# Second token group loads stored low parts of weights, and attention operands take a way through DRAM, in a hybrid decoder layer on one core

## The chip, the cores and the metric

The kernel runs on one core of one Trainium2 chip. The metric is the time of one execution in microseconds (us) on the device.

## What is computed

One decoder layer over 1024 tokens of width 1024 in float32. The part around the change is the mixer: an RMS norm, one projection by `w_in`, four heads of retention and four heads of differential attention, and an output projection. After it comes an expert layer that chooses 16 of 16384 experts for each token and each of eight heads.

```python
h = rmsnorm(x, norm_mix_g); proj = h @ w_in
rq, rk, rv, rg, dq, dk, dv = split(proj)            # dq, dk: 4 heads x 2 maps x 64 columns
q, k as (T, head, map m, 64);  q *= 64 ** -0.5
p_m = softmax(q_m @ k_m.T + alibi, causal);  dy = (p_0 - lam * p_1) @ dv
x = x + concat(silu(rg) * rmsnorm(retention), rmsnorm(dy) * g) @ w_out
x = rmsnorm(x + peer(rmsnorm(x), wq, subkeys, u, v))
```

## The kernel before

The 1024 tokens are eight tiles of 128. `front` runs the mixer and the routing for two groups of tiles after each other: the first group has three tiles (the sparse group: its experts are gathered row by row), the second has five (the dense group: all experts are multiplied). Both groups need the same 52 weight chunks of 128x1024 float32 (512 KB each): 16 for the projections to q and k of the heads (`wt`), 12 to values and gates (`wn`), 8 of `w_out` (`wo`), 16 of the query weights of the routing (`wq`).

Products keep nearly full float32 precision by splitting both factors into a rounded high part and the remainder, the low part, and adding three products. `chunk` (L149) makes the parts of a weight chunk: SyncE (SP) loads `wraw` into one of four buffers (L152), ScalarE (ACT) copies it to the high part `whi` (L154), VectorE (DVE) subtracts to the low part `wlo` (L156). High and low parts have two buffers each (tags `uh` and `ul`). `proj_t` (L168) multiplies a chunk into one PSUM bank (tag `T`, one buffer): 24 matmuls of 384 columns for the first group; for the second 24 matmuls of 320 columns for each of two halves of the tokens, so that the second half waits until the first is read out of the bank. `proj_n` (L178) does the projections whose output has the tokens on the partitions.

For each attention head h, `att_proj` (L295) takes two chunks. A projected half goes to `pt` (one buffer; L300, L316). For q, ACT makes two high parts and their copies in the other 64 partitions (L303, L304) and DVE four low parts (L305, L306): `qa0`, `qa1`, `qb0`, `qb1`. For k, ACT makes the high part (L319) and DVE puts the low part into the other 64 partitions (L320): `kk`. The first group stores its keys to `kd_d` (L323), and the second loads them from GpSimd's (POOL's) queue (L312). `attention` (L327) then handles one tile t after the other: score matmuls `psS` (L343 to L348) into two banks, maxima on DVE (L351, L353), exponentials on ACT (L357), the difference of the two maps on DVE (`e`, L362), transposes `psA` (L369), copies `aT` (L370) and the product with the values `pov` (L373).

L379 to L384 weave the heads: while the tiles of head h run, the four chunks of head h+1 (two of `ret_proj`, L255, whose `qT` is kept in one of two `ga` buffers until the retention of that head is done, and two of `att_proj`) are written in between. While the second group runs, POOL gathers expert rows for the first group (L862), each followed by a multiply on DVE (L864); the place of these on DVE is held back by the list `gates`.

The order of the instructions on each engine is set when the program is built, by a scheduler that weighs program order, free buffers and its own model of durations. At run time every engine, and SP with its transfers, goes through its list strictly in that order, and waits at an instruction whose inputs or buffers aren't ready. A transfer that reads DRAM waits on SP until the store of those bytes has landed.

Of the kernel before, what the change touches and what calls it, by code (L numbers as in the profile page):

```python
# [13 lines left out]
F32 = mybir.dt.float32  # L14
F32R = mybir.dt.float32r
# [4 lines left out]
AF = mybir.ActivationFunctionType  # L20
ALU = mybir.AluOpType
AX = mybir.AxisListType

P = 128
T = 1024
# [3 lines left out]
H = 4  # L29
# [69 lines left out]
def layer_kernel(ctx, tc, x, wt, wn, wo, wq, sk, ut, u, v, gmix, gffn, gfin, gsub, dlam, consts, alb, out):  # L99
# [6 lines left out]
    kd_d = tc.dram_tile([H, 2, P, T], F32, name="kd_d")  # L106
# [27 lines left out]
    def front(m, pp, cst, g0, nt, dense, late):  # L134
# [14 lines left out]
        def chunk(src, shape):  # L149

            raw = wp.tile(shape, F32, tag="raw", bufs=RAW, name="wraw")
            SY.dma_start(raw, src)  # L152
            hi = wp.tile(shape, F32R, tag="uh", bufs=2, name="whi")
            A.activation(hi, raw, AF.Copy)  # L154
            lo = wp.tile(shape, F32R, tag="ul", bufs=2, name="wlo")
            V.tensor_sub(lo, raw, hi.bitcast(F32))  # L156
            return hi, lo
# [83 lines left out]
        yield from proj_n([wn[c] for c in range(4)], hx, lambda t, ps: A.activation(rv[:, t], ps, AF.Copy))  # L241
        yield from proj_n([wn[8 + c] for c in range(4)], hx, put_dv)
# [12 lines left out]
        def ret_proj(h):  # L255
            qT = wp.tile([P, n], F32, tag="ga", bufs=2, name="qT")
            for a, b, ps in proj_t(wt[2 * h], hx):
# [3 lines left out]
            for a, b, ps in proj_t(wt[2 * h + 1], hx):  # L261
                A.activation(kT[:, a:b], ps, AF.Copy, scale=P ** -0.5)
            ops[h] = [qT, kT]
            yield
# [30 lines left out]
        def att_proj(h):  # L295
            qa = [ap.tile([P, n], F32R, tag=f"q2{m}", bufs=2, name=f"qa{m}") for m in range(2)]
            qb = [ap.tile([P, n], F32R, tag=f"qb{m}", bufs=1, name=f"qb{m}") for m in range(2)]
            for a, b, ps in proj_t(wt[8 + 2 * h], hx):
                pt = ap.tile([P, b - a], F32, tag="pt", name="pt")
                A.activation(pt, ps, AF.Copy, scale=0.125)  # L300
                for m in range(2):
                    own, oth = slice(64 * m, 64 * m + 64), slice(64 - 64 * m, 128 - 64 * m)
                    A.activation(qa[m][own, a:b], pt[own], AF.Copy)  # L303
                    A.activation(qa[m][oth, a:b], pt[own], AF.Copy)  # L304
                    V.tensor_sub(qb[m][own, a:b], pt[own], qa[m][own, a:b].bitcast(F32))  # L305
                    V.tensor_sub(qb[m][oth, a:b], pt[own], qa[m][own, a:b].bitcast(F32))  # L306
            yield
            kk2 = ap.tile([P, 2, L], F32R, tag="kd", name="kk") if h % 2 else fp.tile([P, 2, L], F32R, tag="R", name="kk")
            kk = [kk2[:, m] for m in range(2)]
            if not first:  # L310
                for m, tl in enumerate(kk):
                    G.dma_start(tl[:, :lo0], kd_d[h, m][:, :lo0])  # L312
            for a, b, ps in proj_t(wt[8 + 2 * h + 1], hx):
                sl = slice(lo0 + a, lo0 + b)
                pt = ap.tile([P, b - a], F32, tag="pt", name="pt")
                A.activation(pt, ps, AF.Copy)  # L316
                for m in range(2):
                    own, oth = slice(64 * m, 64 * m + 64), slice(64 - 64 * m, 128 - 64 * m)
                    A.activation(kk[m][own, sl], pt[own], AF.Copy)  # L319
                    V.tensor_sub(kk[m][oth, sl], pt[own], kk[m][own, sl].bitcast(F32))  # L320
            if not last:
                for m, tl in enumerate(kk):
                    SY.dma_start(kd_d[h, m][:, lo0:L], tl[:, lo0:].bitcast(F32))  # L323
            ops[h] += [qa, qb, kk]
            yield

        def attention(h):  # L327
# [3 lines left out]
            for t in range(nt):  # L331
# [4 lines left out]
                for m in range(2):  # L336
                    ps = bankA("psS") if both is None else both[:, m:m + 1]
                    ql = slice(t * P, (t + 1) * P)
                    for b in range((Lq + 511) // 512):
                        c0, c1 = b * 512, min(Lq, b * 512 + 512)  # L340
                        o = ps[:, b, :c1 - c0]
                        rl = c0 + T - Lq
                        PE.matmul(o, cst["albl"][:, h], cst["albr"][:, rl:rl + c1 - c0], start=True, stop=False)  # L343
                        diag = c1 == Lq
                        PE.matmul(o, qa[m][:, ql], kk[m][:, c0:c1], start=False, stop=False)
                        PE.matmul(o, qb[m][:, ql], kk[m][:, c0:c1], start=False, stop=not diag)
                        if diag:
                            PE.matmul(o[:, c1 - c0 - P:], identb, cst["mask"], start=False, stop=True)  # L348
# [39 lines left out]
        yield from proj_n([wn[4 + c] for c in range(4)], hx,  # L388
# [14 lines left out]
        for hf in range(2):  # L403
            SY.dma_start(x2[hf], x[g0:g0 + nt, :, 512 * hf:512 * (hf + 1)].rearrange("t p d -> p t d"))
            yield from proj_n([wo[4 * hf + c] for c in range(4)], mx,
# [29 lines left out]
        for hp in range(2 * PH):  # L435
            h = hp // 2
            qT = wp.tile([P, n], F32, tag="ga", bufs=2, name="pqT")
            for a, b, ps in proj_t(wq[hp], nx, "TR"):
                A.activation(qT[:, a:b], ps, AF.Copy)
# [471 lines left out]
```

## Time and profile before

| | |
|---|---|
| time, median of 3 runs | 2898.01 us (2894.97 to 2901.68) |
| time of the profiled execution | 2897.35 us |
| its span | 2895.6 us |
| busy: TensorE (PE), DVE, ACT, POOL | 93%, 82%, 37%, 37% of the span |

The span runs from the first instruction to the last; 1.75 us lie around it. A busy PE is not a PE at its peak: the ends of matmuls are modelled, and overlap. By lines, the execution falls into stages: first group's mixer 0 to 183 us, its routing woven with the second group's first projections to 407 us, the second group's retention and attention to some 690 us, its gate and output projections to 820 us, its routing to 1000 us, one-hot gate tables to 1307 us, and from there the expert loop to the end.

### The profile page before, as it was taken

Reading aid. Unit: us, or ns where it says so; the run is one execution under the profiler, and the core shown is the slowest. Engines: PE = TensorE matmul, PEld = TensorE weight load, DVE = VectorE, ACT = ScalarE, POOL = GpSimd, SP = SyncE. Lnnn points to the kernel's source line nnn. Section 1 sums busy time; section 2 is a strip of 40 time slices with the busy share of each in tenths; the row PEclk is TensorE's granted clock in tenths of the full one; section 3 lists DMA queues with packets and bytes.
Section 4 is the critical chain, followed back from the end, with each engine's and each line's share of the span. In section 5 each row is a group of like instructions: output and inputs, shape, how many; then the busy total and the mean of one; then the engine's idle time right before and its main releaser. Section 6 shows DMA issues by size and latency. Waiting matters only on the chain.

```text
span 2895.6 us, 43107 instructions
## 1 busy us (share of the span) xinstructions
PE 2705.9 (93%) x16043; PEld 2437.2 (84%) x16043; DVE 2362.2 (82%) x4547; ACT 1063.1 (37%) x1881; POOL 1067.1 (37%) x782
## 2 busy tenths in 40 slices
PE   7979987888889999998999999999999999999998
PEld 6868876776789999997887787999999999999987
DVE  3555899878689988985888787888889888988988
ACT  4653334544232369992222222222222222222222
POOL 0000004434310000002555554565565566665664
PEclk9989999999989999999999999999999999999999
DMA  5334236757742246668998898989999999999997
GB/s 170 103 131 141 95 114 230 245 191 241 250 147 82 87 153 238 242 258 298 317 324 301 301 340 307 344 314 353 328 330 348 325 344 339 346 329 332 343 325 259
DMA packets 293238, 742.92 MB, mean 257 GB/s; under 512 B 23450, under 2 KB 117658, under 8 KB 293027
## 3 DMA queue, kind: packets, MB, share of 16 engines
q0 software_dynamic: 111744, 404.28, 39.1%
q1 hardware_dynamic: 181282, 335.88, 33.5%
q8 instruction: 126, 2.06, 0.3%
q14 instruction: 86, 0.70, 0.1%
HBM read 671.71 MB, written 68.35 MB: 256 GB/s over the span
## 4 chain that ended last, share of the span: by engine, by line
PE 34%; DVE 15%; DMA 15%; issue 12%; POOL 7%; ACT 3%; SPq 0%; POOLq 0%; DVEq 0%; ACTq 0%
DMA gl<-hs_d 6%; POOL vg L869 5%; DMA vg<-in_v,idx 4%; DMA ug<-in_u,idx 3%; PE psH L717 3%; PE psH L719 3%; PE psH L718 3%; PE psV L795 3%; PE psV L796 3%; PE psV L797 2%; DVE ug L864 2%; PE psHs L717 2%; PE psHs L719 2%; PE psHs L718 2%; POOL ug L862 2%
## 5 line engine op out<-in xcount | busy, mean ns | idle before, releaser
L869 POOL DMA_INDIRECT vg<-in_v,idx x384 | 548.9, 1429 | 895.3 <-DVE ug L864 521.0
L862 POOL DMA_INDIRECT ug<-in_u,idx x384 | 512.8, 1335 | 499.4 <-DVE ug L864 323.5
L871 DVE SCALAR_TENSOR_TENSOR sa<-vg,shs,sa 128x1024 f32<-128x1024 f32 x384 | 491.7, 1280 | 44.0 <-DMA vg<-in_v,idx 39.2
L864 DVE SCALAR_TENSOR_TENSOR ug<-ug,sx 128x1024 f32<-128x1024 f32 x384 | 460.4, 1219 | 71.0 <-DMA ug<-in_u,idx 70.1
L717 PE MATMUL psH<-nh,uh 128*128 128x320 f32 x1424 | 441.3, 310 | 6.9 <-ACT uh L703 4.8
L718 PE MATMUL psH<-nl,uh 128*128 128x320 f32 x1424 | 440.8, 310 | 0.0
L719 PE MATMUL psH<-nh,ul 128*128 128x320 f32 x1424 | 439.2, 310 | 0.0
L795 PE MATMUL psV<-vh,wh 128*128 128x512 f32 x768 | 305.0, 397 | 26.7 <-DVE accS L831 23.5
L796 PE MATMUL psV<-vl,wh 128*128 128x512 f32 x768 | 303.5, 396 | 0.0
L717 PEld LDWEIGHTS psH<-nh,uh 128*128 128x128 f32 x1424 | 268.6, 189 | 14.2 <-ACT uh L703 5.9
L718 PEld LDWEIGHTS psH<-nl,uh 128*128 128x128 f32 x1424 | 268.6, 189 | 4.9
L719 PEld LDWEIGHTS psH<-nh,ul 128*128 128x128 f32 x1424 | 267.9, 188 | 3.5 <-DVE ul L705 0.2
L720 ACT ACTIVATE ga<-psH 128x320 f32<-128x320 f32 x178 | 75.3, 426 | 411.4 <-PE psH L719 379.6
L703 ACT ACTIVATE uh<-uraw 128x1024 fp32r<-128x1024 f32 x128 | 136.0, 1062 | 214.4 <-PE psH L718 114.9
L717 PE MATMUL psHs<-nh,uh 128*128 128x320 f32 x624 | 197.1, 317 | 9.3 <-ACT ga L720 9.1
L796 PE MATMUL kp<-vl,wh 128*128 128x512 f32 x512 | 200.7, 392 | 2.0 <-DVE vl L819 2.0
L156 DVE TENSOR_TENSOR wlo<-wraw,whi 128x1024 fp32r<-128x1024 f32 x104 | 126.7, 1219 | 92.8 <-ACT whi L154 90.7
L154 ACT ACTIVATE whi<-wraw 128x1024 fp32r<-128x1024 f32 x104 | 110.1, 1058 | 235.1 <-PE psT L162 119.8
L795 PEld LDWEIGHTS psV<-vh,wh 128*128 128x128 f32 x768 | 146.7, 191 | 58.1 <-DVE accS L831 25.3
L718 PE MATMUL psHs<-nl,uh 128*128 128x320 f32 x624 | 195.0, 313 | 0.0
L719 PE MATMUL psHs<-nh,ul 128*128 128x320 f32 x624 | 193.6, 315 | 0.8 <-DVE ul L705 0.8
L795 PE MATMUL kp<-vh,wh 128*128 128x512 f32 x512 | 192.2, 392 | 1.7 <-ACT wh L811 1.7
(251 smaller groups left out, 6250.0 us busy)
## 6 DMA issues: line engine op xcount, KB each, us to landing
uraw<-in_ut SPq DMA_DIRECT2D x128, 512.0 KB
vraw<-in_v SPq DMA_DIRECT2D x128, 512.0 KB
g_d<-st SPq DMA_DIRECT2D x80, 512.0 KB
gt<-g_d SPq DMA_DIRECT2D x32, 1280.0 KB
wraw<-in_wt SPq DMA_DIRECT2D x32, 512.0 KB
wraw<-in_wq SPq DMA_DIRECT2D x32, 512.0 KB
hs_d<-ga SPq DMA_DIRECT2D x39, 320.0 KB
gl<-hs_d SPq DMA_DIRECT2D x39, 320.0 KB
```

Source lines behind the costliest of these rows:

```text
L154: A.activation(hi, raw, AF.Copy)
L156: V.tensor_sub(lo, raw, hi.bitcast(F32))
L703: A.activation(uh, raw, AF.Copy)
L717: PE.matmul(ps, uh[:, dc], xh[:, dc, sl], start=(dc == 0), stop=False)
L718: PE.matmul(ps, uh[:, dc], xl[:, dc, sl], start=False, stop=False)
L719: PE.matmul(ps, ul[:, dc], xh[:, dc, sl], start=False, stop=(dc == DC - 1))
L795: PE.matmul(ps, Wh[e][:, sl], Vh[e][:, so], start=start, stop=False)
L796: PE.matmul(ps, Wh[e][:, sl], Vl[e][:, so], start=False, stop=False)
L862: G.indirect_dma_start(out=ug, out_offset=None, in_=u, in_offset=bass.IndirectOffsetOnAxis(ap=idxA[t][:, k:k + 1], axis=0))
L864: gate(V.scalar_tensor_tensor(ug, ug, 1.0, xt, op0=ALU.mult, op1=ALU.mult, accum_out=hs[:, k:k + 1]))
L869: G.indirect_dma_start(out=vg, out_offset=None, in_=v, in_offset=bass.IndirectOffsetOnAxis(ap=idxA[t][:, k:k + 1], axis=0))
L871: gate(V.scalar_tensor_tensor(ac, vg, hs[:, k:k + 1], ac, op0=ALU.mult, op1=ALU.add))
```

## The change

The first group stores each low part to DRAM (`wl_d`) after the subtraction; the second group loads it, into the same two buffers, and does no subtraction. `chunk` takes the number of a chunk in place of its address. The projected q and k of attention are split once, at full width, by one ACT copy and one DVE operation that both read PSUM, into a tile `st`; it goes to DRAM (`qk_d`), and six loads of 64 partitions form `qa`, `qb` and `kk` from there. `kd_d` and the loads on POOL's queue go. `st` has one buffer (`pt`) in the first group, and takes the two `ga` buffers, which `qT` uses too, in the second.

```diff
-        def chunk(src, shape):
+        def chunk(i, shape):
             raw = wp.tile(shape, F32, tag="raw", bufs=RAW, name="wraw")
-            SY.dma_start(raw, src)
+            SY.dma_start(raw, wsrc[i])
             hi = wp.tile(shape, F32R, tag="uh", bufs=2, name="whi")
+            lo = wp.tile(shape, F32R, tag="ul", bufs=2, name="wlo")
+            flat = lo.bitcast(F32).rearrange("p a b -> p (a b)")
+            if not first:
+                SY.dma_start(flat, wl_d[i])
             A.activation(hi, raw, AF.Copy)
-            lo = wp.tile(shape, F32R, tag="ul", bufs=2, name="wlo")
-            V.tensor_sub(lo, raw, hi.bitcast(F32))
+            if first:
+                V.tensor_sub(lo, raw, hi.bitcast(F32))
+                SY.dma_start(wl_d[i], flat)
             return hi, lo
...
         def att_proj(h):
-            qa = [ap.tile([P, n], F32R, tag=f"q2{m}", bufs=2, name=f"qa{m}") for m in range(2)]
-            qb = [ap.tile([P, n], F32R, tag=f"qb{m}", bufs=1, name=f"qb{m}") for m in range(2)]
-            for a, b, ps in proj_t(wt[8 + 2 * h], hx):
-                pt = ap.tile([P, b - a], F32, tag="pt", name="pt")
-                A.activation(pt, ps, AF.Copy, scale=0.125)
-                for m in range(2):
-                    own, oth = slice(64 * m, 64 * m + 64), slice(64 - 64 * m, 128 - 64 * m)
-                    A.activation(qa[m][own, a:b], pt[own], AF.Copy)
-                    A.activation(qa[m][oth, a:b], pt[own], AF.Copy)
-                    V.tensor_sub(qb[m][own, a:b], pt[own], qa[m][own, a:b].bitcast(F32))
-                    V.tensor_sub(qb[m][oth, a:b], pt[own], qa[m][own, a:b].bitcast(F32))
...
+            for i, scale in ((0, 0.125), (1, 1.0)):
+                for a, b, ps in proj_t(WT + 8 + 2 * h + i, hx):
+                    if first:
+                        st = ap.tile([P, 2, b - a], F32R, tag="pt", name="st")
+                    else:
+                        st = wp.tile([P, 2, b - a], F32R, tag="ga", bufs=2, name="st")
+                    A.activation(st[:, 0], ps, AF.Copy, scale=scale)
+                    V.scalar_tensor_tensor(st[:, 1], ps, scale, st[:, 0].bitcast(F32), op0=ALU.mult, op1=ALU.subtract)
+                    SY.dma_start(qk_d[h, i][:, :, lo0 + a:lo0 + b].rearrange("s p t -> p s t"), st.bitcast(F32))
+                yield
+            qa, qb = (ap.tile([P, 2, n], F32R, tag=tg, bufs=nb, name=tg) for tg, nb in (("q20", 2), ("qb", 1)))
+            kk = ap.tile([P, 2, L], F32R, tag="kd", name="kk") if h % 2 else fp.tile([P, 2, L], F32R, tag="R", name="kk")
+            lo, hi = slice(0, 64), slice(64, 128)
+
+            def part(i, s, c0):
+                return qk_d[h, i, s][:, c0:L].rearrange("(m p) t -> p m t", m=2)
+            for tl, rows, src in ((qa, lo, part(0, 0, lo0)), (kk, lo, part(1, 0, 0)), (kk, hi, part(1, 1, 0)),
+                                  (qa, hi, part(0, 0, lo0)), (qb, lo, part(0, 1, lo0)), (qb, hi, part(0, 1, lo0))):
+                SY.dma_start(tl.bitcast(F32)[rows], src)
             ops[h] += [qa, qb, kk]
-            yield
```

What this does to the order is seen at three places of the second group's attention, between head 0 and head 1. The first is PE at the transposes of tile 3 of head 0 (`psA` of the exponentials `e0`). Before (`psT_4366` and `psT_4391` are the two halves of the projection of head 1's k):

```order
L163 MATMUL psT_4366<-hh_1608,wlo_4364 128x320
L277 MATMUL ret_4292<-pack_66,kT_3651 128x128
L280 MATMUL ret_4292<-rv_2082,am_4294 128x128
L282 MATMUL ret_4292<-S_83,qT_3556 128x128
L284 MATMUL ret_4292<-rv_2082,kn_4297 128x128
L369 MATMUL psA_4335<-pack_66,e0_4325 128x128 x4
L369 MATMUL psA_4341<-pack_66,e0_4325 128x128 x3
L161 MATMUL psT_4391<-hh_1608,whi_4362 128x320
L162 MATMUL psT_4391<-hl_1609,whi_4362 128x320
L163 MATMUL psT_4391<-hh_1608,wlo_4364 128x320
```

And now, from the same transposes on (line numbers are those of the changed kernel: eight more than before up to `att_proj`, two less from `attention` on; `psS_4567` is the first score tile of head 1, of which only the position term is done here):

```order
L371 MATMUL pov_4188<-dvh_3949,aT_4177 128x128 x2
L281 MATMUL ret_4291<-qT_3585,kT_3680 128x128
L367 MATMUL psA_4334<-pack_67,e0_4324 128x128 x4
L367 MATMUL psA_4340<-pack_67,e0_4324 128x128 x3
L371 MATMUL pov_4345<-dvh_3949,aT_4333 128x128 x4
L341 LDWEIGHTS ab_191
L341 MATMUL psS_4567<-ab_191 128x512
L285 MATMUL ret_4291<-pack_67,kT_3680 128x128
```

The projections that stood on both sides of the transposes are gone from there: from the scores of tile 2 to the last `pov` of tile 4 the list has none, and the second half of head 1's q, both halves of its k and the retention chunks of head 2 follow in one row behind the head. Tiles 0 and 1 still have projections between them.

The second place is ACT where the halves of head 1's attention projections are read out of PSUM, with what each instruction waits for. Before (`pt_4253` is the second half of q, `pt_4416` the first of k):

```order
L300 ACTIVATE pt_4253<-psT_4218 128x320 [waits DVE_49]
L303 ACTIVATE qa0_4183<-pt_4253 64x320 [waits Activation_49]
L304 ACTIVATE qa0_4183<-pt_4253 64x320
L303 ACTIVATE qa1_4184<-pt_4253 64x320
L304 ACTIVATE qa1_4184<-pt_4253 64x320
L279 ACTIVATE kn_4297<-ret_4292,c_kdec_185 128x128 [waits PE_49]
L316 ACTIVATE pt_4416<-psT_4366 128x320 [waits DVE_49,Activation_49]
```

Now (`st_4258` is the second half of q, `st_4412` and `st_4416` are those of k, `qT_4505` is the retention's q of head 2; DMAHW3 and DMAHW6 count the completion of the store of the `st` tile before):

```order
L310 ACTIVATE st_4258<-psT_4229 128x320 [waits DMAHW3_49]
L298 ACTIVATE jk_4502,msr_3583<-ret_4491,c_cross_184 128x128 [waits DVE_49]
L300 ACTIVATE rv_2095<-ret_4491,c_cross_184 128x128 [waits PE_49]
L310 ACTIVATE st_4412<-psT_4362 128x320 [waits DMAHW6_49,DVE_49,PE_49]
L287 ACTIVATE kn_4606<-ret_4601,c_kdec_186 128x128 [waits PE_49]
L161 ACTIVATE whi_4618<-wraw_4616 128x1024 [waits DMAHW2_49,PE_49]
L310 ACTIVATE st_4416<-psT_4387 128x320 [waits DMAHW3_49,DVE_49,PE_49]
L266 ACTIVATE qT_4505<-psT_4512 128x320 [waits DMAHW6_49,DVE_49,PE_49]
```

The wait on DVE's subtractions is replaced by one on the landing of the store of the half before, since one `ga` buffer is held by `qT` and the other is shared by these four halves and the next `qT`.

The third place is SP's list over the same time. Before, it has mostly loads of raw chunks there:

```order
L152 DMA wraw_4505<-in_wt 128x1024 [waits DMAHW1_49,DVE_49]
L858 DMA sa_24095<-x2_d_58 128x1024 [waits DVE_49]
L152 DMA wraw_4615<-in_wt 128x1024 [waits DMAHW2_49,DMAHW0_49,DVE_49]
L856 DMA sx_24093<-xn_d_57 128x1024 [waits DVE_49]
L152 DMA wraw_4787<-in_wt 128x1024 [waits DMAHW4_49,DVE_49]
```

Now, from the store of the second half of head 1's q on (`wlo_4619` is the low part of a chunk of the retention of head 2):

```order
L312 DMA qk_d_60<-st_4258 128x2x320 [waits DVE_49]
L322 DMA q20_4482<-qk_d_60 64x2x640 [waits DMAHW7_49,DMAHW6_49,DMAHW3_49]
L322 DMA q20_4482<-qk_d_60 64x2x640 [waits DMAHW0_49]
L322 DMA qb_4483<-qk_d_60 64x2x640 [waits DMAHW1_49]
L322 DMA qb_4483<-qk_d_60 64x2x640 [waits DMAHW2_49]
L312 DMA qk_d_60<-st_4412 128x2x320 [waits DVE_49]
L160 DMA wlo_4619<-wl_d_61 128x1024 [waits DMAHW4_49,PE_49]
L155 DMA wraw_5173<-in_wt 128x1024 [waits DMAHW5_49,Activation_49]
L312 DMA qk_d_60<-st_4416 128x2x320 [waits DVE_49]
L322 DMA kk_4484<-qk_d_60 64x2x1024 [waits DMAHW7_49,DMAHW6_49,DMAHW3_49]
L322 DMA kk_4484<-qk_d_60 64x2x1024 [waits DMAHW0_49]
```

SP now holds stores, loads that wait for those stores to land, and loads of low parts that wait until PE has freed a buffer, in one list.

## Rows read from the trace of the kernel before

**Rows 1.** The page, busy time and share of the span.

```profile
PE 2705.9 (93%) x16043; PEld 2437.2 (84%) x16043; DVE 2362.2 (82%) x4547; ACT 1063.1 (37%) x1881; POOL 1067.1 (37%) x782
```

**Rows 2.** Windows: stretch, us, busy PE, PEld, DVE, ACT, POOL, PEclk, DMA share, GB/s.

```profile
60.00:183.00 123.00, 112.98 (x679) 102.21 (x678) 61.00 (x125) 70.23 (x190) 0.00 (x0) 1.00 0.30 103
407.00:440.00 33.00, 26.21 (x170) 24.33 (x168) 32.42 (x81) 14.38 (x29) 2.35 (x4) 1.00 0.28 88
440.00:510.00 70.00, 54.59 (x343) 48.13 (x341) 63.55 (x119) 29.34 (x73) 35.28 (x31) 0.90 0.71 243
510.00:575.00 65.00, 57.85 (x381) 51.13 (x382) 56.52 (x103) 32.65 (x89) 29.68 (x27) 0.97 0.74 247
575.00:641.00 66.00, 58.24 (x387) 52.28 (x386) 49.51 (x90) 31.93 (x80) 22.40 (x19) 0.95 0.56 185
641.00:690.00 49.00, 34.47 (x198) 27.59 (x197) 40.68 (x79) 23.27 (x69) 22.16 (x18) 0.86 0.66 222
720.00:820.00 100.00, 80.31 (x362) 65.97 (x361) 68.37 (x122) 31.35 (x58) 32.22 (x25) 0.88 0.69 242
820.00:1000.00 180.00, 176.46 (x1227) 173.66 (x1226) 168.78 (x1037) 55.27 (x103) 3.54 (x3) 1.00 0.27 90
1000.00:1307.00 307.00, 295.06 (x2718) 283.65 (x2718) 265.43 (x384) 255.13 (x427) 0.00 (x0) 0.99 0.57 214
1307.00:2895.00 1588.00, 1539.14 (x8232) 1375.42 (x8231) 1348.84 (x1600) 397.35 (x562) 903.13 (x639) 0.99 0.92 325
```

**Rows 3.** Windows of L161 alone: busy PE, PEld, PEclk, DMA share, GB/s.

```profile
575.00:641.00 66.00, 22.20 (x66) 13.11 (x65) 0.95 0.56 185
641.00:690.00 49.00, 0.09 (x1) 0.00 (x0) 0.86 0.66 222
```

**Rows 4.** Waits of PE in 440:641: total us, times, longest.

```profile
PE psA L369 <- DVE e L362: 11.5, 4, 4.3
PE psT L161 <- ACT pt L300: 9.7, 2, 7.2
```

**Rows 5.** Waits of PE in 641:690.

```profile
PE ret L277 <- DVE am L275: 8.1, 2, 5.6
```

**Rows 6.** Groups by form in 400:720: count, busy us, mean ns, idle before.

```profile
L156 DVE TENSOR_TENSOR wlo<-wraw,whi 128x1024 fp32r<-128x1024 f32 x20 | 24.3, 1217 | 5.4 <-ACT whi L154 5.4
...
L320 DVE TENSOR_TENSOR kk<-pt,kk 64x320 fp32r<-64x320 f32 x16 | 7.8, 490 | 0.5
L306 DVE TENSOR_TENSOR qb<-pt,qa 64x320 fp32r<-64x320 f32 x16 | 7.8, 486 | 0.2
...
L305 DVE TENSOR_TENSOR qb<-pt,qa 64x320 fp32r<-64x320 f32 x16 | 7.7, 482 | 0.2
...
L300 ACT ACTIVATE pt<-psT 128x320 f32<-128x320 f32 x8 | 3.5, 435 | 13.0 <-DVE qb L306 9.0 <-PE psT L163 3.9
...
L362 DVE SCALAR_TENSOR_TENSOR e<-e,rz,e 128x512 f32<-128x512 f32 x4 | 3.0, 752 | 0.0
```

**Rows 7.** Timeline of PE in a projection: start, us, engine, line.

```profile
435.30 0.31 PE L161 MATMUL psT<-hh,whi 128*128 128x320 f32 x1
...
437.06 0.31 PE L161 MATMUL psT<-hh,whi 128*128 128x320 f32 x1
```

**Rows 8.** Chain that ended last, transfers in it: start, us, what.

```profile
1171.96 6.14 DMA hs_d<-ga
...
1324.30 8.29 DMA hs_d<-ga
1332.61 4.61 DMA gl<-hs_d
...
2884.49 2.64 DMA out<-fin
```

**Rows 9.** The page, DMA issues: count, KB each.

```profile
hs_d<-ga SPq DMA_DIRECT2D x39, 320.0 KB
...
out<-fin SPq DMA_DIRECT2D x5, 512.0 KB
```

More of the change, by code (lines that the diff above doesn't have):

```diff
@@ L105, in layer_kernel @@
     hs_d = tc.dram_tile([SPILL, P, TB], F32, name="hs_d")
-    kd_d = tc.dram_tile([H, 2, P, T], F32, name="kd_d")
+    qk_d = tc.dram_tile([H, 2, 2, P, T], F32, name="qk_d")
+    wl_d = tc.dram_tile([52, P, D], F32, name="wl_d")
+    wsrc = [w[i] for w, k in ((wt, 16), (wn, 12), (wo, 8), (wq, 16)) for i in range(k)]
+    WT, WN, WO, WQ = 0, 16, 28, 36
     dv_d = tc.dram_tile([NT, P, H * P], F32, name="dv_d")
@@ L239, in put_dv @@
             SY.dma_start(dv_d[g0 + t], dvt)
-        yield from proj_n([wn[c] for c in range(4)], hx, lambda t, ps: A.activation(rv[:, t], ps, AF.Copy))
-        yield from proj_n([wn[8 + c] for c in range(4)], hx, put_dv)
+        yield from proj_n([WN + c for c in range(4)], hx, lambda t, ps: A.activation(rv[:, t], ps, AF.Copy))
+        yield from proj_n([WN + 8 + c for c in range(4)], hx, put_dv)
         yield "projected"
@@ L256, in ret_proj @@
             qT = wp.tile([P, n], F32, tag="ga", bufs=2, name="qT")
-            for a, b, ps in proj_t(wt[2 * h], hx):
+            for a, b, ps in proj_t(WT + 2 * h, hx):
                 A.activation(qT[:, a:b], ps, AF.Copy)
@@ L260, in ret_proj @@
             kT = ap.tile([P, n], F32, tag="kT", bufs=2, name="kT")
-            for a, b, ps in proj_t(wt[2 * h + 1], hx):
+            for a, b, ps in proj_t(WT + 2 * h + 1, hx):
                 A.activation(kT[:, a:b], ps, AF.Copy, scale=P ** -0.5)
@@ L307, in att_proj @@
-            yield
[L308 to L320, printed above, removed]
@@ L321, in att_proj @@
-            if not last:
-                for m, tl in enumerate(kk):
-                    SY.dma_start(kd_d[h, m][:, lo0:L], tl[:, lo0:].bitcast(F32))
+            for i, scale in ((0, 0.125), (1, 1.0)):
[8 more added lines that the diff above has]
+                yield
@@ L324, in att_proj @@
             ops[h] += [qa, qb, kk]
-            yield
         def attention(h):
@@ L344, in attention @@
                         diag = c1 == Lq
-                        PE.matmul(o, qa[m][:, ql], kk[m][:, c0:c1], start=False, stop=False)
-                        PE.matmul(o, qb[m][:, ql], kk[m][:, c0:c1], start=False, stop=not diag)
+                        PE.matmul(o, qa[:, m, ql], kk[:, m, c0:c1], start=False, stop=False)
+                        PE.matmul(o, qb[:, m, ql], kk[:, m, c0:c1], start=False, stop=not diag)
                         if diag:
@@ L387, in front @@
         rg = fp.tile([P, nt, 512], F32, tag="R", name="rg")
-        yield from proj_n([wn[4 + c] for c in range(4)], hx,
+        yield from proj_n([WN + 4 + c for c in range(4)], hx,
                           lambda t, ps: A.activation(rg[:, t], ps, AF.Silu))
@@ L404, in front @@
             SY.dma_start(x2[hf], x[g0:g0 + nt, :, 512 * hf:512 * (hf + 1)].rearrange("t p d -> p t d"))
-            yield from proj_n([wo[4 * hf + c] for c in range(4)], mx,
+            yield from proj_n([WO + 4 * hf + c for c in range(4)], mx,
                               lambda t, ps: V.tensor_add(x2[hf][:, t], ps, x2[hf][:, t]))
@@ L437, in front @@
             qT = wp.tile([P, n], F32, tag="ga", bufs=2, name="pqT")
-            for a, b, ps in proj_t(wq[hp], nx, "TR"):
+            for a, b, ps in proj_t(WQ + hp, nx, "TR"):
                 A.activation(qT[:, a:b], ps, AF.Copy)
```

## The prediction

> **What bounds the kernel now.** I read the page first, then windows by stage, then the waits of PE in the stages that the change touches, then the durations of what is removed, and last the transfers that stand on the chain that ended last. PE is busy for 93% of the span [rows 1]. The windows show where it is the bound and where not [rows 2]: in the second group's routing (820 to 1000) it is busy for 176.46 of 180 us, in the gate tables for 295.06 of 307, in the expert loop for 1539.14 of 1588. Work taken from DVE there buys nothing, because PE has no idle time to give back. The change edits nothing after 1000 us, and I find the order there unchanged, so those 1895 us should stay as they are. What is left is the front, where PE sits idle for 10 of 123 us (60 to 183), 6.8 of 33 (407 to 440), and in the second group's four heads 15.4, 7.2, 7.8 and 14.5 us (440 to 690). These 45 us of idle PE are both the most that the change can win in the heads and the baseline for what it can lose.
>
> Heads 0 to 2 and head 3 differ in one thing. In heads 0 to 2 the projections of the next head stand between the tiles; in head 3 there are none left, as L161 alone shows: 66 matmuls in 575 to 641, one in 641 to 690 [rows 3]. So head 3 is what a head costs without filler: 14.5 us of idle PE for five tiles, 2.9 us a tile, since the chain maximum, exponential, difference, transpose, copy is then in the open. PE's waits agree: in heads 0 to 2 it waits 11.5 us for DVE's `e` and 9.7 us for `pt` to be read [rows 4], in head 3 8.1 us for DVE's `am` [rows 5].
>
> **The change part by part.** *Taken from DVE and ACT.* In 400 to 720 there are 20 subtractions of 1217 ns for low parts (24.3 us), and 23.3 us of `qb` and `kk` [rows 6]. In place of the latter come 16 operations of 128x320 out of PSUM; the rows nearest are 64x320 from SBUF at 0.48 us and 128x512 at 0.75 us, and I take 0.6 (9.6 us in all; the ends give 7.7 to 12). DVE gets 38 us lighter, 16% of the 243 us that it is busy in 407 to 690. What that is worth is bounded by PE's waits for DVE there, 11.5 and 8.1 us: nothing at one end, 19.6 us at the other. I take 16% of them, 3 us, because what DVE is late with is mostly the tile's own chain and the gathered rows in its list, which stay. ACT also loses work, but PE waits for it mainly at `pt`, counted below.
>
> *Filler moved.* By the order, tiles 2 to 4 of heads 0 to 2 now have no projection beside them; tiles 0 and 1 keep theirs. Three unfilled tiles cost 8.7 us of idle PE a head (three fifths of head 3's 14.5). Tiles 0 and 1 keep two fifths of today's idle time without the waits for `pt`: (30.3 - 9.7) / 3 x 0.4, or 2.7 us.
>
> *The moved projections.* Behind the head stand six halves in a row. Within a half matmuls start 0.147 us apart (the two rows of L161 stand twelve matmuls apart [rows 7]), so a half is 3.5 us, six 21.1 us. Four halves, those of q and k, now share one free buffer: each is read out by ACT (0.435 us), then DVE (0.6), then stored, and the next can't be read out before that store has landed, nor can the PSUM bank be used again. The trace has no store of `st`; the row nearest is `hs_d<-ga`, also 320 KB [rows 9], on the chain once with 6.14 us and once, under heavier traffic, with 8.29; the 512 KB of `out<-fin`, with nothing beside them, took 2.64 [rows 8]. I take 6.14: DMA share is 0.57 in that store's stage and 0.56 to 0.74 in the heads, against 0.92 in the loop [rows 2]. A cycle is then 7.2 us against 3.5 of matmuls. Four cycles and the load of `kk` back (I take `gl<-hs_d`, 4.61 us [rows 8]) are 33.3 us. Beside it PE has the six halves and some 3 us of retention (an estimate, under half of head 3's 6.9 busy us a tile), 24 us: 9.3 us idle. Ahead of head 3 only three halves and two steps of retention are left (some 16.6 us): 16.7 us idle.
>
> The heads then cost 20.7, 20.7 and 28.1 us of idle PE, 69.5 against 30.3: **+39 us**. Head 3 itself stays as it is. With the store at 2.64 the cycle is 3.7, the chain 19.3, and only 2.7 us show, ahead of head 3: 36.9, +7. With 8.29 it is 9.3, the idle times are 17.9 and 25.3, in all 95: +65.
>
> One sentence from the Trainium skill speaks against 6.14: DMA: Bandwidth & Descriptors, "Anatomy of one DMA", fits 2.0 us plus bytes over 436,000 for transfers issued by GpSimd, by which 320 KB would take an estimated 2.75 us, the heads would cost about +7 us, and the kernel would hardly be slower. The rows here say more than twice that for a store of the same size [rows 8], and the measurement decides.
>
> *The start of the second group* (407 to 440): the same four cycles ahead of head 0, 9.3 us idle by the same working against 6.8 today [rows 2]: **+2.5**. DVE is busy for 32.4 of these 33 us, so the release may come later still.
>
> *First group's heads.* Here a half has 384 columns, 4.2 us by columns. `st` has one buffer, so k's read-out waits for q's store: 0.435 x 1.2 + 0.6 + a store. DMA share is only 0.30, so I go nearer to 2.64, to 4.6 (about the middle of 2.64 and 6.14): 5.7 against 4.2 and a step of retention. **+2**, bounds 0 and +8. The 52 stores of low parts are covered: such a buffer is wanted again two chunks later, over 8 us, and the store takes 8.29 at worst.
>
> *Gate and output chunks of the second group* (690 to 820). A low part's buffer comes free at the end of the chunk before last; its load then has one chunk of PE to hide behind, 30 matmuls of 512 columns, 7.05 us by columns. At 6.14 it is hidden, at 8.29 it shows by 1.2 us in each of 12 chunks. The two loads of 1280 KB for the residual stand ahead of one of them. **+3**, bounds -2.5 and +15. In the routing (820 to 1000) the same load has 48 x 0.147 = 7.05 us and more, at DMA share 0.27: 0. If that cover were gone, 16 chunks would show up to 1.2 us each.
>
> *POOL's queue* loses the eight loads of `kd_d`; gathers go on as before, since their places on DVE count the same up to the end of the heads (83 gathers in both orders). 0.
>
> Sum: 39 + 2.5 + 2 + 3 - 3 = 43.5 us on the profiled execution's 2897.35 us: **2941 us**. That execution lies 0.66 us below the median shown, which changes nothing.
>
> **The rivals.** *Stores land fast, DVE decides.* If a store of `st` lands in under about 3 us, the four cycles all but hide behind their matmuls, and what counts is the lighter DVE: +7 for the heads, -19.6 if all of PE's waits for DVE go, -3.7 at the start, where PE's waits for `pt` fall away: about -16, **2881 us**. For it: 2.64 us for a store on an empty queue, and kernels bound by a chain through DVE. Against it: share 0.56 to 0.74 in this stretch, and tiles 2 to 4 in the open whatever the stores do.
>
> *Traffic makes every transfer late.* Low parts (20 x 512 KB in the heads' stretch) and q and k (some 3.7 MB a head) add about 24 MB to some 65 MB between 440 and 720 (232 GB/s in the mean), all from SP's list, where a load that waits for a store holds up everything behind it. With 8.29 us: +65 in the heads, +11 at the start, +15 in the chunks, +8 in the first group, -3: **2993 us**. A rule of the Trainium skill leads the same way: DMA: Bandwidth & Descriptors, "Rules for kernel authors", says that two transfers to disjoint halves of the partitions serialize, and to use one of 128 partitions. No row here shows such a pair. For the rival as a mechanism of this kernel: `kk` comes as two loads, and if they add up, the load is 9.2 us in place of 4.61, 4.6 more in each of four heads.
>
> *It cancels.* With 4.61 us for a store a cycle is 5.6, the chain 27.2, idle 3.2, 3.2 and 10.6: +21 in the heads, -3.6 at the start; the lighter DVE returns up to 19.6 more: **2897 us** with the small terms, no change. Also what would be seen if the built order mattered less than it looks, because PE's idle time only changes its place.
>
> **How the numbers follow.** A difference under 0.2%, some 6 us, can't be told from no change, since the runs before lie 0.23% apart. My forecast gets 58%, with a range of its own of 2915 to 2970 (store at 5 to 7.2 us); fast stores 15%, late traffic 15%, cancelling 12%. The range 2888 to 2985 leaves out most of the first and the far half of the second. Faster gets the fast stores and a little of the cancelling, 16%; same 10%; slower 74%.
>
> **What would show it.** Right: the score matmuls of head 3 start some 40 us later than 641; PE waits for ACT's read-out of `st`, and ACT for the store of `qk_d`, 5 to 7 us at a time; idle PE in the heads near 85 us; the expert loop takes 1588 us as before. Wrong: ACT hardly waits for stores; idle PE in the heads at 45 us or less; the gate and output chunks or the first group carry the difference, or the loop's length moves.

## The result and the profile after

The changed kernel takes 2979.39 us (median of 4 runs, 2971.01 to 2981.94) against 2898.11 us of the kernel before, run beside it: a ratio of 1.028, 95% interval 1.0258 to 1.0302. It is slower by 81 us; 2941 was forecast, with a range of 2888 to 2985. In the profiled executions the span grows from 2895.6 to 2979.3 us, by 83.7 us.

The page, busy time as in [rows 1], and the queue of SyncE's transfers (packets, MB, share of the 16 engines; before 335.88 MB and 33.5%):

```profile
PE 2725.1 (91%) x16043; PEld 2448.4 (82%) x16043; DVE 2282.3 (77%) x4447; ACT 1033.2 (35%) x1810; POOL 1065.9 (36%) x774
...
q1 hardware_dynamic: 208546, 411.39, 40.3%
```

DVE is 80 us lighter, PE has the same 16043 instructions and is busy for 19 us more. To find the place, I cut both traces where the same number of matmuls is done. Idle PE is the length of a stretch less PE's busy time in it. Two windows of the kernel before, in the columns of [rows 2]:

```profile
280.00:407.00 127.00, 115.28 (x639) 105.38 (x638) 105.98 (x629) 39.74 (x61) 0.00 (x0) 1.00 0.32 109
407.00:721.00 314.00, 262.36 (x1627) 229.70 (x1626) 268.51 (x526) 143.86 (x360) 127.50 (x109) 0.94 0.64 217
```

The windows of the changed kernel that answer to them, then the second of them in pieces (to head 0's first score, head by head, and to 779 for head 3), the gate and output projections, and the expert loop:

```profile
297.00:424.00 127.00, 115.28 (x638) 105.08 (x637) 99.34 (x631) 39.91 (x62) 0.00 (x0) 1.00 0.58 200
424.00:810.00 386.00, 280.05 (x1625) 239.46 (x1625) 233.36 (x470) 123.66 (x312) 118.47 (x101) 0.89 0.72 236
...
424.00:490.00 66.00, 42.05 (x235) 39.65 (x234) 46.87 (x106) 12.42 (x22) 19.80 (x15) 0.87 0.73 239
490.00:580.00 90.00, 65.94 (x385) 56.93 (x385) 51.38 (x96) 27.84 (x74) 33.02 (x27) 0.87 0.81 270
580.00:662.00 82.00, 62.74 (x388) 54.32 (x389) 44.81 (x84) 28.51 (x75) 22.72 (x21) 0.92 0.75 234
662.00:741.00 79.00, 49.53 (x319) 41.99 (x319) 42.52 (x80) 26.69 (x72) 19.97 (x19) 0.88 0.71 229
741.00:779.00 38.00, 31.11 (x156) 22.84 (x157) 27.91 (x52) 16.75 (x47) 10.02 (x9) 0.79 0.31 99
810.00:893.00 83.00, 65.51 (x292) 51.98 (x291) 46.37 (x87) 22.64 (x38) 26.38 (x22) 0.92 0.82 299
1390.00:2979.00 1589.00, 1538.04 (x8232) 1373.58 (x8232) 1349.66 (x1600) 398.73 (x564) 912.64 (x639) 0.99 0.92 325
```

The first group's routing is the same 127 us with the same 115.28 us of busy PE, but it stands 17 us later: that much was lost in the first group. The stretch from there to the second group's mixed rows grows from 314 to 386 us, by 72: idle PE from 51.6 to 105.9 us, and the same matmuls are busy for 17.7 us longer, at a mean granted clock of 0.89 in place of 0.94, between the levels of 1.2 and 2.4 GHz, with more idle time among them; busy time multiplied by the clock is nearly equal in the two (246.6 and 249.2). The gate and output projections last 72 us in both traces (first transposes of the mixed rows at 721.3 and 809.9, of the normed rows at 793.4 and 882.2), and the loop 1589 us against 1588.

The chain that ended last shows the step ahead of head 0 (start, us, what):

```profile
457.36 12.28 DMA qk_d<-st
...
469.75 0.45 ACT st L310
...
470.22 0.50 DVE st L311
...
470.74 7.33 DMA qk_d<-st
...
478.12 0.58 SPq L322
...
478.76 11.30 DMA kk<-qk_d
...
490.19 0.48 PE psS L343
```

A store, the read-out that waited for its buffer, the next store, the load of `kk`, the first score. The same pieces stand ahead of the other heads (scores at 580.6, 662.0 and 741.5 us; in the kernel before 510.0, 575.9 and 641.6). Waits in 424 to 779, of PE and then of ACT:

```profile
PE psT L169 <- DVE st L311: 27.1, 5, 9.0
PE psS L343 <- DMA kk<-qk_d: 24.1, 4, 19.7
...
ACT st L310 <- DMA qk_d<-st: 23.3, 5, 7.0
...
ACT qT L266 <- DMA qk_d<-st: 14.6, 2, 8.0
```

PE waits 27.1 us for the PSUM bank to be read out (9.7 us in 440 to 641 of before [rows 4]), and 24.1 us for `kk`, a wait that no row of before has; ACT waits for stores 37.9 us. DMA issues in 440 to 810 (count, KB each, median us from issue to landing):

```profile
wlo<-wl_d SPq DMA_DIRECT2D x18, 512.0 KB, 7.1
qk_d<-st SPq DMA_DIRECT2D x16, 320.0 KB, 6.2
...
kk<-qk_d SPq DMA_DIRECT2D x8, 512.0 KB, 8.9
...
qb<-qk_d SPq DMA_DIRECT2D x8, 320.0 KB, 9.4
```

### The profile page after: what moved, and what is told of

The parts are those of the page before. It is cut to its first block, busy times and chain, and to the rows that moved or that the text cites. A ratio compares the mean times of both kernels' runs of the same rounds, so it can differ in the third digit from the quotient of the medians.

```text
span 2979.3 us, 43215 instructions
## 1 busy us (share of the span) xinstructions
PE 2725.1 (91%) x16043; PEld 2448.4 (82%) x16043; DVE 2282.3 (77%) x4447; ACT 1033.2 (35%) x1810; POOL 1065.9 (36%) x774
## 4 chain that ended last, share of the span: by engine, by line
PE 49%; DMA 16%; DVE 10%; issue 6%; ACT 3%; POOL 2%; SPq 0%; DVEq 0%; POOLq 0%; ACTq 0%
DMA gl<-hs_d 6%; PE psH L716 5%; PE psH L715 5%; PE psH L717 5%; PE psV L793 3%; PE psV L794 3%; PE psV L795 3%; DMA qk_d<-st 3%; DVE sa L869 2%; PE psHs L715 2%; PE psHs L717 2%; PE psHs L716 2%; PE kp L794 2%; PE kp L795 2%; PE kp L793 2%
## 5 line engine op out<-in xcount | busy, mean ns | idle before, releaser
L869 DVE SCALAR_TENSOR_TENSOR sa<-vg,shs,sa 128x1024 f32<-128x1024 f32 x384 | 491.5, 1280 | 41.6 <-DMA vg<-in_v,idx 37.8
L161 ACT ACTIVATE whi<-wraw 128x1024 fp32r<-128x1024 f32 x104 | 110.0, 1058 | 282.2 <-PE psT L170 155.7
L703 DVE TENSOR_TENSOR ul<-uraw,uh 128x1024 fp32r<-128x1024 f32 x128 | 156.0, 1219 | 44.9 <-ACT uh L701 44.5
## 6 DMA issues: line engine op xcount, KB each, us to landing
gt<-g_d SPq DMA_DIRECT2D x32, 1280.0 KB, 17.4
```

The lines of the kernel that those rows point to most:

```text
L703: V.tensor_sub(ul, raw, uh.bitcast(F32))
L869: gate(V.scalar_tensor_tensor(ac, vg, hs[:, k:k + 1], ac, op0=ALU.mult, op1=ALU.add))
```

## The experiments

Theory 1: the chain of store, store and load costs nearly all, and low parts are neutral. Rival A: the low parts' traffic makes all transfers late. Rival B: the order costs it, since projections no longer stand beside the tiles. "Late" is how much later than in the kernel before the first group's routing stands (448 weight-chunk products done, 393.2 us there); the stretch is 407 to 721 of before and the same products in the others (1613 to 1647 matmul records). The kernels were timed on four occasions, on which the kernel before took 2891 to 2898 us, so a difference between two medians of different occasions is uncertain by some 7 us.

| kernel | median us | ratio (95%) | late | stretch | busy PE | idle PE | clock |
|---|---|---|---|---|---|---|---|
| before | 2891 to 2898 | 1 | 0 | 314 | 262.4 | 51.6 | 0.94 |
| after | 2979.4 | 1.0280 (1.0258 to 1.0302) | 16 | 386 | 280.1 | 105.9 | 0.89 |
| low parts alone | 2871.4 | 0.9906 (0.9887 to 0.9925) | 7 | 296 | 257.8 | 38.2 | 0.97 |
| low parts of 40 chunks | 2867.4 | 0.9911 (0.9891 to 0.9930) | 0 | 292 | 257.9 | 34.1 | 0.95 |
| low parts, GpSimd stores | 2875.0 | 0.9932 (0.9910 to 0.9954) | 11 | 290 | 253.2 | 36.8 | 0.99 |
| no second subtract | 2859.8 | 0.9882 (0.9861 to 0.9903) | 0 | 300 | 262.2 | 37.8 | 0.96 |
| operands alone | 2985.5 | 1.0308 (1.0292 to 1.0324) | 30 | 391 | 282.6 | 108.4 | 0.88 |
| own store buffers | 2937.9 | 1.0142 (1.0120 to 1.0164) | 13 | 347 | 272.8 | 74.2 | 0.89 |
| old planes | 2934.1 | 1.0129 (1.0103 to 1.0155) | 16 | 356 | 273.1 | 82.9 | 0.89 |
| both | 2917.7 | 1.0072 (1.0050 to 1.0095) | 18 | 329 | 270.2 | 58.8 | 0.90 |
| keys early | 2907.8 | 1.0039 (1.0020 to 1.0057) | 16 | 320 | 270.4 | 49.6 | 0.91 |
| first group on chip | 2956.6 | 1.0212 (1.0189 to 1.0236) | 4 | 386 | 280.9 | 105.1 | 0.88 |

**Low parts alone.** `chunk` is that of the changed kernel; against the kernel before, `att_proj` only takes its chunks by number:

```diff
...
-            for a, b, ps in proj_t(wt[8 + 2 * h], hx):
+            for a, b, ps in proj_t(WT + 8 + 2 * h, hx):
...
```

> The stored and reloaded low parts alone; attention operands as before the change. Theory 1 (the serial chain store, store, read-out of the attention operands costs nearly all of the +81 us): 2898 to 2918 us, the later start of the first group's heads (10 to 25 us in the trace after) being the most that this part can carry; in the second group's heads no wait on a store, scores of head 3 less than 25 us after the 641 us of before. Rival A (the 26 MB that the low parts add each way make every transfer late): 2945 to 2980 us, most of the loss, and the heads of the second group as late as after the change.

Faster than the kernel before by 23 us, which neither theory had. Rival A falls: with 52 stores and 52 loads there the heads are not late but early, head 3's scores at 632.5 us. Its windows:

```profile
287.00:414.00 127.00, 115.28 (x639) 105.28 (x638) 99.30 (x628) 39.86 (x61) 0.00 (x0) 1.00 0.58 201
414.00:710.00 296.00, 257.77 (x1616) 225.11 (x1626) 246.73 (x507) 144.89 (x360) 129.90 (x109) 0.97 0.76 264
```

The routing of the first group is 7 us late, the stretch 18 us shorter, with 21.8 us less of busy DVE. So 11 us of the gain are there at the end of the stretch; of the 25 us between the two spans the others come behind it, 4 in the second group's routing and some 7 in the expert loop, which has no edit.

**Operands alone.** In both groups:

```diff
+            A.activation(hi, raw, AF.Copy)
             lo = wp.tile(shape, F32R, tag="ul", bufs=2, name="wlo")
-            flat = lo.bitcast(F32).rearrange("p a b -> p (a b)")
-            if not first:
-                SY.dma_start(flat, wl_d[i])
-            A.activation(hi, raw, AF.Copy)
-            if first:
-                V.tensor_sub(lo, raw, hi.bitcast(F32))
-                SY.dma_start(wl_d[i], flat)
+            V.tensor_sub(lo, raw, hi.bitcast(F32))
```

> The split at full width with store and read-out of the attention operands alone; low parts of the weights subtracted in both groups as before. Theory 1: 2955 to 2975 us, scores of the second group's head 3 at 715 to 740 us, and stores still 5 to 10 us long. Rival A: without the low parts' traffic the stores fall to about 4 us and the time to 2905 to 2930 us.

91 us slower than before, more than the whole change, and 10 us above theory 1's range; head 3's scores start at 761.3 us. Rival A falls here too: without the low parts' traffic nothing comes back. The two parts don't add up (91 - 23 = 68 against 81), but their signs are clear. The first group is 30 us late here, more than with the low parts' stores beside it (16). Most of that stands in its heads, where PE waits 17.4 us for `kk` (95 to 200 us), against 2.1 after the change (95 to 186); why the transfers stand later here is open.

**Own store buffers.**

```diff
-                        st = wp.tile([P, 2, b - a], F32R, tag="ga", bufs=2, name="st")
+                        st = ap.tile([P, 2, b - a], F32R, tag="pt", bufs=2, name="st")
...
-            qa, qb = (... (("q20", 2), ("qb", 1)))
+            qa, qb = (... (("q20", 2 if first else 1), ("qb", 1)))
...
-                cd = fp.tile([P, nt, NC2], F32, tag="q20", bufs=2, name="cd")
+                cd = fp.tile([P, nt, NC2], F32, tag="q20" if first else "pt", bufs=2, name="cd")
```

> The changed kernel, but in the second group the tile between split and store has two buffers of its own, and no longer the one that the retention query leaves it (room for them from the second buffer of the attention query, whose next load comes after the last use of the first anyway). Theory 1: the wait of ScalarE for the store before falls from about 38 us to under 10, and 25 to 45 us of the 81 come back (2935 to 2955 us). Rival B (not the stores but the order costs it: the work that filled the gaps now stands ahead of the read-outs instead of beside the tiles): under 15 us come back, since the read-outs still stand behind the last tile of the head before.

41 us come back, as theory 1 had it, 39 of them in the stretch, and ACT waits for no store any more. Ahead of head 0 nothing is gained: 66 us from the start of the stretch to the first score, as after the change.

**Old planes.**

```diff
             def part(i, s, c0):
-                return qk_d[h, i, s][:, c0:L].rearrange("(m p) t -> p m t", m=2)
+                hd = h if first or not h else h - 1
+                return qk_d[hd, i, s][:, c0:L].rearrange("(m p) t -> p m t", m=2)
```

> The changed kernel, but heads 1 to 3 read the planes of the head before instead of their own (the attention output is then that of other operands), so that no read-out has to wait for a store that was just issued; sizes, counts and order of all transfers stay. Theory 1: the last store drops out of the chain ahead of heads 1 to 3, about 6 to 10 us for each head in the second group and less in the first, 20 to 40 us back (2940 to 2960 us). Rival A (traffic): nothing back, 2970 to 2985 us. Rival B (order): under 10 us back.

45 us come back, more than theory 1's 20 to 40, with every transfer kept: what costs is the chain of waits, not the bytes. Their order, which the expectation takes as kept, is another, though. With no store in front, the loads of head 1's `kk` stand beside those of head 0 (480 to 482 us), and those of heads 2 and 3 are issued 13 and 24 us ahead of these heads' first scores. So this run takes the load of `kk` off the chain together with the wait for the store, and does not split the two; PE waits for `kk` no more. The edit touches the second group alone. Of the 45 us the stretch shows 30; most of the rest lies in the expert loop, whose products `psV`, first to last, took 1528 us in this execution and 1529 to 1547 in the others, without any edit there.

**Both.** The two edits above together.

> Own store buffers in the second group and, in heads 1 to 3, the planes of the head before (so the attention output is that of other operands): neither the wait for the buffer nor the wait for a fresh store is left; all transfers stay. Buffers alone brought 41 us back, old planes alone 45. If these are two links of one chain after each other, they add: 2885 to 2905 us. If both only relieve the same late transfer, the time stays at 2920 to 2940 us.

In between: 62 of 41 + 45 us come back, 57 in the stretch of 39 + 30. The two edits relieve links of one chain, with a smaller overlap. Against low parts alone 33 us are left in the stretch. About half of it lies ahead of head 0, whose planes are fresh in this kernel too: 62 us from the start of the stretch to the first score against 32, of which some 14 us are 31 chunk products (93 matmuls at 0.147 us [rows 7]) that now stand there and no longer in the heads. The other half is in the heads, where the loads of the query planes now stand on the chain, in buffers that the last tile of the head before must release (the chain; start, us, what):

```profile
531.96 18.90 DMA qb<-qk_d
...
591.42 12.17 DMA q<-qk_d
...
651.40 12.80 DMA qb<-qk_d
```

**Keys early.** On top of the own buffers, with the query loads in a step of their own:

```diff
-            nxt = chain(ret_proj(h + 1), att_proj(h + 1)) if h < H - 1 else iter(())
+            nxt = chain(att_proj(h + 1), ret_proj(h + 1), att_q(h + 1)) if h < H - 1 else iter(())
```

> The changed kernel with the store buffers of its own in the second group, and for each head (in both groups) the attention projections ahead of the retention projections, with the loads of kk issued between the two and those of the query planes behind them: two weight chunks of projection stand between the last store and the scores. Theory 1: the stores and the loads of kk lie beside projections, 10 to 30 us faster than with buffers alone: 2905 to 2928 us. Rival B (the read-outs stand behind the head's last tile whatever they wait for): within 8 us of the 2938 us with buffers alone.

Another 30 us back: in place of rival B's nothing, but only because the order was changed. Two chunks of projection behind the stores cover most of the store and the load of `kk`: PE's wait for `kk`, 24.1 us after the change, is gone. Order is a part of the cost, then, by what stands between a store and its reader.

**First group on chip.**

```diff
+        att = att_proj if first else att_proj2
+        yield from att(0)
...
+            for m in range(2):
+                SY.dma_start(kk.bitcast(F32)[:, m, :lo0], kd_d[h, m][:, :lo0])
```

> The changed kernel, but the first group forms its attention operands on chip as before the change and stores its key columns for the second group as before; only the second group stores planes and reads them out (its earlier key columns come in two loads of their own). This splits the operands' cost by group. In the trace after, the first group's norm2 transposes end 17.5 us later than before, of which the low parts alone show 8. Theory 1 (the cost lies mostly in the second group's heads): 8 to 15 us back, 2962 to 2972 us. Rival: the first group's round trips carry a third of the loss or more, 25 us or more back, under 2955 us.

23 us come back by the medians, between the two. But the kernel before was 7 us faster on this occasion (2891.2 us); against it the loss is 65 us in place of 81, so 16 us come back (20 by the ratios in the table), just above theory 1's 8 to 15. The traces show the same: the routing of the first group is 12 us earlier than after the change, the stretch is unchanged at 386 us, and 11 us lie in the expert loop, within its variation above. So the operands cost some 12 us in the first group, and the low parts the rest of the 16.

**No second subtract.**

```diff
+            if not first:
+                return hi, hi
             lo = wp.tile(shape, F32R, tag="ul", bufs=2, name="wlo")
```

> The kernel before, where the second group's low parts are neither subtracted nor loaded (the high part takes their place in the product, with as many matmuls on TensorE; the output lacks that correction). Theory: the 23 us that the low parts alone gained come from the 52 subtracts of VectorE in the second group; without the stores and loads that pay for them the gain is larger, 2855 to 2872 us. Rival: the gain came from another order of the program, and the subtracts cost nothing, as the prediction took them (3 us): 2885 to 2897 us.

35 us faster than before, with a stretch of 300 us: the 52 subtracts do hold up the second group. By the spans, 41 us apart, 15 are there at the end of the stretch, 9 come in the gate and output projections (63 us in place of 72), 4 in the second group's routing, and most of the rest in the expert loop, which has no edit. The stores and loads of the low parts cost some 12 of the 35; 8 of them lie in the gate and output projections, which take 71 us with the low parts alone.

**Low parts, GpSimd stores.** Against low parts alone:

```diff
-                SY.dma_start(wl_d[i], flat)
+                G.dma_start(wl_d[i], flat)
```

> The low parts alone, their stores issued from GpSimd's queue in place of SyncE's. With stores on SyncE the second group's first transposes began 210.0 us after the start, 12 us later than before, and TensorE waited 9.4 us there for the normed input, whose load stands in SyncE's queue behind stores that wait for VectorE. Theory: 5 to 10 us of this come back, 2861 to 2867 us. Rival (the traffic itself delays the first group): 2868 to 2875 us.

The rival's time. TensorE waits the same 9.4 us for the normed input as with low parts alone (there, group of the first transposes in 150 to 215: count, busy us, mean ns, idle before):

```profile
L217 PE MATMUL psX<-pack,xt 128*128 128x128 f32 x16 | 4.2, 427 | 9.8 <-DVE xt L235 9.4 <-ACT yd L384 0.4
```

**Low parts of 40 chunks.** Against low parts alone:

```diff
+            kept = not (WN + 4 <= i < WN + 8 or WO <= i < WQ)
-            if not first:
+            if not first and kept:
                 SY.dma_start(flat, wl_d[i])
             A.activation(hi, raw, AF.Copy)
-            if first:
+            if first or not kept:
                 V.tensor_sub(lo, raw, hi.bitcast(F32))
+            if first and kept:
                 SY.dma_start(wl_d[i], flat)
```

> The low parts alone, but not for the 12 gate and output chunks, whose low parts both groups subtract as before: 40 stores and 40 loads. With all 52 the second group's first transposes are 12 us later than before, right behind those 12 stores. Theory (these stores delay the normed input): the first transposes return to within 4 us of 198 us and the time falls to 2860 to 2867 us. Rival (the traffic over the whole first group, or the order there): transposes still at 205 us or later, 2868 to 2876 us; if the second group needs its 12 subtracts gone, above 2876 us.

The same group, in the same stretch:

```profile
L219 PE MATMUL psX<-pack,xt 128*128 128x128 f32 x16 | 4.4, 431 | 3.9 <-DVE hl L222 2.8 <-ACT yd L386 1.1
```

The wait is gone and these transposes begin at 194.8 us, within 0.5 us of before; those of the second tile, which the two expectations count, begin at 198.5 us (198.0 before, 210.0 with low parts alone). So the 12 stores between the groups delay the input, by whichever queue; the reason given ahead of the run before, their place in SyncE's list, does not hold, and how they delay it is open. The time, 0.9% below before, lies just above the theory's upper end and can't be told apart from low parts alone. The three kernels with stored low parts and without stored operands beat both the kernel before and the changed one.

## Why the prediction was right, and where its sizes were off

*Direction and mechanism: right.* The serial chain of store, read-out, store and load stands on the path ahead of every head, ACT waits for stores up to 7.0 and 8.0 us at a time, and the loop kept its length. Old planes and own buffers together took its waits away, and with them most of the heads' loss (first score to mixed rows 266.6 us, against 319.7 after the change and 263.7 with low parts alone).

*The size: too small.* The time lies above the forecast's own range of 2915 to 2970, and nearer the second rival's 2993 than 2941; only the wider range holds it. Head 3's scores start 100 us later than before, not some 40: 16 us in the first group, 36 from there to head 0's first score, 48 in heads 0 to 2. The rival's cause, the low parts' traffic, fell with operands alone, but its prices for a store and for `kk` were the better ones, as follows.

*The heads, 39 - 3 = +36 us of idle PE: right as a sum, not in its terms.* 490 to 779 has 79.7 us of idle PE (289 - 209.3), near the 85 that were to show, against 44.9 in 440 to 690 [rows 2]. That is in part luck. Between the heads (537 to 580.6, 634 to 662, 716 to 741.5) PE is idle for 46.5 us, where 9.3, 9.3 and 16.7 were forecast; beside the tiles of heads 0 to 2 it is idle for 26.7 us in place of 34.2, and head 3, which was to stay at 14.5, falls to 6.9. And the heads alone, first score to mixed rows, became 37 us longer (282.9 to 319.7) as the difference of +56 (operands, against the 263.7 of low parts alone) and -19 (low parts).

*The DVE term, 3 us, failed.* I took 16% of PE's waits for DVE [rows 4, 5] and wrote that what DVE is late with mostly stays. Taking the second group's subtracts away shortened the stretch by 14 us and the kernel by 35, low parts with their traffic by 18 and 23. The wait list names the last releaser of each wait; the chain of the kernel before, in 440 to 721, has its share in DVE's list and what that list waits for:

```profile
by line: issue 24.6%; DMA ug<-in_u,idx 19.4%; DVE ug L864 10.2%; POOL ug L862 8.7%; PE psT L161 3.9%; DVE Z L351 3.9%; PE psT L162 3.6%; PE psT L163 3.5%; PE pov L373 2.7%; PE psS L345 1.9%; PE psS L346 1.8%; PE psS L343 1.7%; DVE e L362 1.
```

Gathered rows and a tile's maximum, exponential difference and mask product share one list, so a subtract that leaves it moves everything behind it up; this way of the gain is argued from the chain, the gain itself is measured. The first rival's lighter DVE, 19.6 us, was the better term; what fell was its condition, that stores land in under 3 us.

*The store, 6.14 us: right in the median,* 6.2 over 16 in 440 to 810, but nine of them on the chain between 457 and 734 took 5.19 to 12.28 us, 8.4 in the mean, near the second rival's 8.29: the late ones set the end. Why they are late is open; with the operands alone the stores on the chain took 5.16 to 11.30 us too. *The load of `kk`, 4.61 us: failed.* I took a load of 320 KB [rows 8, 9]; `kk` is two of 512 KB, and the later ones took 11.30, 9.87, 8.87 and 7.01 us on the chain, 2.4 to 6.7 us a head over the forecast.

*The start of the second group, +2.5: failed.* 424 to 490 has 24 us of idle PE against 6.8 in 407 to 440 [rows 2], +17. The last store there and the load of `kk` are long (12.28, 7.33 and 11.30 us in a row); own buffers and old planes leave most of it, since head 0 reads planes just stored.

*The granted clock: no term of the sum had it.* The stretch's matmuls were busy 17.7 us longer at 0.89 than at 0.94. So the idle time that was priced came with slower matmuls that were not. Idle time in all does not fix that clock: keys early had 0.91 with 49.6 us of idle PE, before 0.94 with 51.6.

*The first group, +2: failed,* 17 us. The store itself was right (4.7 us in the median over 8 in 60 to 200; 4.6 was taken), but I priced a store against its cover and not the chain, and took the low parts' stores as covered; 12 of them stood ahead of the second group's input. *Gate and output chunks, +3:* no change, 72 us in both; what their loads cost (8 us by low parts alone against no second subtract), the subtracts gave back (9 us). *The routing, 0:* it is 3 us shorter, 4 with the low parts alone.

In all: 17 (first group) + 17 (start) + 35 (heads) + 2 (idle PE in the rest of the stretch) + 18 (clock) makes 89; the stages behind are some 5 us shorter, which leaves the 83.7 of the spans.

The Trainium skill's DMA: Bandwidth & Descriptors, "Rules for kernel authors", has it that two transfers to disjoint partition halves serialize. The trace agrees. Ahead of head 3 the two halves of `kk` are the only transfers, in 733 to 742 of the changed kernel (40 slices of 0.225 us: busy tenths of the 16 engines, GB/s; then count, KB each, median us to landing):

```profile
DMA  2000000009510599999999899999998710000000
GB/s 85 11 0 0 0 0 0 0 0 218 36 18 18 200 455 364 273 200 218 182 219 200 164 273 237 237 218 200 218 200 164 128 18 0 0 0 0 0 0 0
...
kk<-qk_d SPq DMA_DIRECT2D x2, 512.0 KB, 6.2
```

The first lands 5.3 us after its issue at 733.75, the second 7.01 us after its own at 734.38, so 7.6 us go by for the pair. The pair's 32 packets of 4 bytes, 16 for each half and one for each engine, stand 16 between 737.5 and 738.5 us and 16 from 739.5 us on, which reads as one half after the other. The engines are busy all the while and move some 200 GB/s, where they moved some 400 for the stores of 512 KB from 128 partitions, also alone, at the end of the kernel before (`out<-fin`, 2886 to 2888 us). The four pairs took 12.0, 10.5, 9.5 and 7.6 us from the first issue to the last landing, 9.9 in the mean. With other transfers beside it, then, the pair took longer than alone; the rival's 9.2 us for it was near, and the forecast's 4.61 was half of what came. No run here loads `kk` in one transfer of 128 partitions, so what that would save is not shown.

## What to carry to other kernels

A change made of two parts can hold a gain and a loss: cost and time them apart. Here the part that frees the engine whose list is the chain gains about 1% alone, and the other, a trip through DRAM between a product and its use, loses 3%. Put a trip through DRAM where other work stands between the store and its reader, give what is stored a buffer of its own, and size a load by its bytes, and by the number of transfers it comes in, before taking a row for it. Where PE becomes idle, look for a lower granted clock of the matmuls around it too.

## What the runs showed of the hardware

Loads of 320 KB into 64 partitions took 12.17 to 18.90 us on the chain with both waits removed, two to three times the 6.2 us of a store of the same size in the changed kernel, while the 16 engines were busy for 0.84 of that stretch. With low parts alone the granted clock was 0.97 in the stretch, with the attention operands 0.88 to 0.91 in every variant, also where idle PE was as short as before (49.6 us, keys early). The `psV` products of the expert loop, the same code in all kernels, took 1528 to 1547 us in one execution of each of the twelve. While the two halves of `kk` were the only transfers, the 16 engines were busy and moved some 200 GB/s, against some 400 for stores of 512 KB from 128 partitions.
